# Expanding layer B's bias rows from the second pair of layer A on, and moving their last four transfers in SyncE's queue

## The chip, the cores and the metric

The kernel runs on one core of a Trainium2 chip. A core has TensorE (matmuls, PE in the profile, with its weight loads shown apart as PEld), VectorE (DVE), ScalarE (ACT), GpSimd (POOL) and SyncE (SP), which issues the DMA transfers here; the transfers run on 16 DMA engines. The metric is the time of one execution on the device in microseconds; lower is better.

## The reference

A block of two layers over 512 tokens of width 1024, 16 heads of 64. Each layer normalises x, multiplies it by one large weight matrix, mixes tokens, multiplies by silu of a gate and by an output matrix, and adds the result to x.

```python
for i in range(DEPTH):                      # DEPTH = 2
    hn = rms_norm(x, norm_gain[i])
    if i % 2 == 0:
        y = mixer_a(hn, a_w_in, a_w_out, a_q_gain, a_k_gain, t5_bias)
    else:
        y = mixer_b(hn, b_w_in, b_w_out, b_q_gain, b_k_gain, b_rpb)
    x = x + y
```

Layer A's mixer is attention over three dilated windows, whose outputs are merged by their softmax denominators; layer B's is attention of each token to its neighbours on an 8 x 64 grid. Both add a learned bias to the scores. Layer B's:

```python
bias = col_bias[:, row_idx].transpose(0, 2, 3, 1, 4)
logits = jnp.einsum('bhcqd,bhrcjd->bhcqrj', qr, kr) + bias
logits = jnp.where(col_valid[:, :, None, :], logits, NEG_INF)
p = jax.nn.softmax(logits...)
out = jnp.einsum('bhcqrj,bhrcjd->bhcqd', p, vr)
```

The bias depends on the distance of a query and a key in rows and columns, not on their places, so a table of 15 x 31 numbers for a head has to be spread out into one row for each query.

## The kernel before, in words

Float32 is kept by splitting every weight and activation into two parts (wh and wl, hn_h and hn_l) and summing three matmuls for each product (mm3). Weights stream in: wraw loads (L199, 512 KB each) go through SyncE's queue, ScalarE casts each to wh (L141), and VectorE or GpSimd subtracts for wl (L147, in split).

Layer A works on heads in eight pairs, hc = 0 to 7 in the code. While TensorE projects pair hc + 1 (main_a), the attention of pair hc (attn_a) is slipped in between, in two halves, u = 0 and u = 1. Each half forms scores (tiles called log) in four PSUM banks, takes exponentials, and VectorE transposes P in blocks into a tile tr (L905). A transfer writes tr to DRAM (td, L914) and four transfers read it back in order into pt (L918): that is P^T. The first half's reads fill half of pt, the second half's the rest. The products P^T V (weigh, tiles called o) follow once for the pair, in the first half of the next pair's attention; they need all eight reads. They take their two PSUM banks from the same four that the scores use, in turn, so pair 5's products use the banks of the first two score tiles of pair 6. The queries and keys of a pair make a similar trip through DRAM (qd, L716; qt, L723), and so does V (vd, L638; vv, L642). For pair 7 there is no such trip; pair 6's projection leaves the gate to later, so pair 5's second half has fewer matmuls behind it than that of other pairs.

The order on TensorE is written out by hand; the other engines' instructions follow the order in which the code emits them, or a scheduler's. What is to be issued at a later place is handed to later_on (L248) with a delay, counted in a running estimate of TensorE's time; tick emits it when the estimate gets there. So a transfer's place in SyncE's queue comes from such a delay. SyncE issues in order: what stands behind an issue that waits, waits too.

Layer A's bias for a pair is loaded by bias_a (tiles e, L877), a pair ahead. Layer B's bias is prepared during layer A by bias_rows (L465), which is called at the end of the first half of pair 2: it loads the table (rp, L468), GpSimd negates it (L469) and lays a copy with a border of large numbers (lb, L471 and L472), and two transfers write these to DRAM (gb_d, lb_d, L473 and L474). Fourteen transfers (spread_out, L486) expand the rows into ex_d, and four (in_order, L490, 640 KB each) copy them into the order in which layer B's bias_b reads them (eb_d). All eighteen are handed to later_on, 10500 apart from 30000 on.

Of the kernel before, what the change touches and what calls it, by code (L numbers as in the profile page):

```python
# [59 lines left out]
def tile_hybrid_encoder(  # L60
# [187 lines left out]
    def later_on(delay, job):  # L248

        timers.append((clock[0] + delay, job))  # L250
        timers.sort(key=lambda t: t[0])
# [123 lines left out]
    def row_scale(ssq):  # L375

        rsqrt(nc.vector, rs_n, ssq, 4, 1.0 / D)
# [28 lines left out]
    def gains():  # L406
        nc.sync.dma_start(hg, head_gain)
        nc.gpsimd.tensor_copy(ng.rearrange("p l k -> p (l k)"), x_ng[:, : 2 * KT])
        for i, (a, b) in enumerate(((0, 3), (1, 4), (2, 5), (6, 7))):
            m = nc.vector.scalar_tensor_tensor(  # L410
                gk[:, i : i + 1], hg[:, a : a + 1], -SCALE, hg[:, b : b + 1], op0=ALU.mult, op1=ALU.mult
            )
            tc.keep_in_program_order(m)

    def scales_a():
        pa = spread()
        nc.scalar.mul(trj(rs_half), to_trj(pa), 0.5)

    def norm(layer, k, xk):

        g = (ng if layer else x_ng[:, : 2 * KT].rearrange("p (l k) -> p l k", l=2))[:, layer, k : k + 1]
        h, l = hn_h[:, k, :], hn_l[:, k, :]
        nc.scalar.activation(h, xk, AF.Copy, scale=g)  # L423
        return nc.vector.scalar_tensor_tensor(l, xk, g, h.bitcast(F32), op0=ALU.mult, op1=ALU.subtract)

    def square_a(k):
        nc.scalar.activation(x_of(k), x_of(k), AF.Square)

    def row_sums(ssq):

        pk = bank("pk")
        for t in range(4):
            matmul(pk[:, t : t + 1], ssq[:, P * t : P * t + P], ones.bitcast(F32)[:, 0:1], start=True, stop=True)
        return pk[:, 0:4]

    def bias_lines():

        t5 = wk.tile([16, LINE], F32, tag="tr", name="t5", bufs=1)
        tc.keep_in_program_order(nc.sync.dma_start(t5, t5x))
        mk = wk.tile([16, LINE], F32, tag="q12", name="mk", bufs=1)  # L440
        nc.sync.dma_start(mk, maskc)
        nc.vector.tensor_sub(mk, mk, t5)
        nc.sync.dma_start(line_d[:, :384], mk[:, :384])
        nc.sync.dma_start(lines_d.rearrange("h g c -> h (g c)"), mk[:, 384:])

        def spread_out(dst, src):
            tc.keep_in_program_order(nc.sync.dma_start(dst, src))

        line = lambda o, *dims: bass.AP(line_d.tensor, line_d.offset + o, [[448, 16], *dims])
        fars = lambda o, *dims: bass.AP(lines_d.tensor, lines_d.offset + o, [[448, 32], *dims])  # L450
        far = l12_d.rearrange("h g r c -> (h g) r c")
        jobs = [
            (l0_d[:, 32 * j + 8 * s : 32 * j + 8 * s + 8, :], line(127 - j - 4 * s, [-16, 8], [1, 256]))
            for j in range(4)
            for s in range(4)
        ]
        jobs += [
            (far[:, 8 * s : 8 * s + 8, 56 * k : 56 * k + 56], fars(64 * (3 - s + k) + 7, [-1, 8], [1, 56]))
            for s in range(4)
            for k in range(4)  # L460
        ]
        for n, job in enumerate(jobs):
            later_on(3000 + 500 * n, partial(spread_out, *job))

    def bias_rows():  # L465

        rp = wk.tile([P, 248], F32, tag="eg", name="rp")
        tc.keep_in_program_order(nc.sync.dma_start(rp, rpb))  # L468
        nc.gpsimd.tensor_scalar(rp, rp, -1.0, None, op0=ALU.mult)  # L469
        lb = wk.tile([P, 376], F32, tag="eg", name="lb")  # L470
        nc.gpsimd.memset(lb, BIG)  # L471
        nc.gpsimd.tensor_copy(lb[:, 15 * 8 : 31 * 8], rp[:, 7 * 8 : 23 * 8])  # L472
        nc.sync.dma_start(gb_d, rp)  # L473
        nc.sync.dma_start(lb_d, lb)  # L474

        far, near = (lb_d, 376), (gb_d, 248)
        jobs = [(2 * W5 + W5 * n, W5, far, 120) for n in range(4)]
        jobs += [(o, 32, far, 24) for o in (0, W5, 7 * W5 - 32, 8 * W5 - 32)]
        jobs += [(32, 32, near, 216), (64, 96, near, 120), (W5 + 32, P, near, 88)]
        jobs += [(6 * W5, P, near, 56), (7 * W5, 96, near, 56), (7 * W5 + 96, 32, near, 24)]  # L480

        def spread_out(o, n, src, at):
            t, width = src
            dst = bass.AP(ex_d.tensor, ex_d.offset + o, [[4 * EB, P], [EB, 4], [1, n]])
            src = bass.AP(t.tensor, t.offset + at, [[width, P], [-8, 4], [1, n]])
            tc.keep_in_program_order(nc.sync.dma_start(dst, src))  # L486

        def in_order(c):
            dst = eb_d.rearrange("h (c r) x -> c h r x", c=4)[c]
            tc.keep_in_program_order(nc.sync.dma_start(dst, ex_d[:, c].rearrange("(h r) x -> h r x", h=16)))  # L490

        jobs = [partial(spread_out, *job) for job in jobs] + [partial(in_order, c) for c in range(4)]
        for n, job in enumerate(jobs):
            later_on(30000 + 10500 * n, job)

    st = {}
    pq = wk.tile([P, 4096], F32, tag="pt", name="pt", bufs=1)
# [373 lines left out]
    def bias_a(hc):  # L871
        e0 = wk.tile([P, 2, 256], F32, tag="e0", name="e0")
        e12 = wk.tile([P, 4, 224], F32, tag="e12", name="e12")
        hs = slice(2 * hc, 2 * hc + 2)

        def load(dst, src):
            tc.keep_in_program_order(nc.sync.dma_start(dst, src))  # L877

        load(e0, l0_d[hs].rearrange("h p c -> p h c"))
        for j in range(4):  # L880
            load(e12[32 * j : 32 * j + 32], l12_d[hs].rearrange("h g r c -> r (h g) c"))
        return e0, e12
# [471 lines left out]
    def side():  # L1354
        for k in range(KT):
            norm(0, k, x_of(k))
            if k:
                square_a(k - 1)
            stamp["na", k] = 0
            if k == 4:  # L1360
                gains()
            yield 1000
        square_a(KT - 1)
        for k in range(1, KT):
            yield 1300
            nc.vector.tensor_add(x_of(0), x_of(0), x_of(k))
        yield 1500
        row_scale(row_sums(x_of(0)))
        yield 2500
        bias_lines()  # L1370
        later_on(21000, lambda: st.__setitem__(("e", 0), bias_a(0)))
        yield 2500
        scales_a()
        first_out()
        stamp["rs", "a"] = 0
        halves = []
        for hc in range(NHC):
            if hc < NHC - 1:
                yield from q_a(hc)
                if hc:  # L1380
                    yield from halves.pop(0)
                yield from st.pop(("land", hc))()
                half = attn_a(hc)
                for v in half:
                    if v == "half":
                        if hc == 2:
                            bias_rows()
                        halves.append(half)
                        break
                    yield v  # L1390
            else:
                gap[0] = cycle((500, 500, 700))
                yield from halves.pop(0)
                yield from chain(q_a(hc), k_a(hc))
                yield from attn_a(hc)
        yield from residual(xg, 0)
        yield from residual(xg, 4)
        stamp["ya", KT - 1, "y"] = 0
        yield "wait", ("x", KT - 1), 800
        for f in range(KT):  # L1400
            square_b(f)
            yield 600
        yield 4500
        row_scale(row_sums(st.pop("ssq")))
        stamp["rs", "b"] = 0
        yield 5000
        nc.scalar.mul(rs_half, spread(), 0.5)
        stamp["rs", "all"] = 0
        for job, hc, delay in B_PLAN:
            yield "wait", ("b", "start"), delay  # L1410
            if job == "scores":
                yield from side_b(hc)
                continue
            if hc == NHC - 1:
                yield "wait", ("back", hc), 0
                yield from residual(xm_d, 0)
            yield "wait", ("back", hc), 3500
            if hc == NHC - 2:
                stamp["yb", "turned"] = 0
            pending.pop(0)()  # L1420
            if hc == NHC - 1:
                stamp["yb", "last"] = 0
            yield
            if hc == NHC - 1:
                yield from residual(xm_d, 4)

    run(main(), side())


# [101 lines left out]
```

## Time and profile before

| | |
|---|---|
| time, median of 3 runs | 808.53 us (807.92 to 809.21) |
| the profiled execution | 808.45 us |
| its span, first to last instruction | 806.7 us |
| TensorE busy | 798.6 us (99%) |
| VectorE, ScalarE, GpSimd busy | 526.6, 442.6, 222.2 us |
| mean granted clock of TensorE | 0.996 |
| moved by DMA | 174.76 MB, 217 GB/s on average |
| the rows of layer B's bias, expanded (L486) | issued from 258.2 to 401.2 us |
| their four transfers into read order (L490) | issued from 412.6 to 454.1 us |
| layer B's first read of them (L889) | 561.2 us |

All of a profile's times are from one execution; a time that stands alone is counted from the span's start. A row of a timeline begins with the start and the duration, then the engine, the line, the operation, what is written and read, and a count; in brackets stands how long the engine was idle before it and what the profile takes for the releaser, the event that ended the wait. SPq marks an issue by SyncE: its row is the time of issuing, not of the transfer. How long a transfer took to land, from its issue on, stands in the rows of DMA issues, with its size. The windows view gives the busy time of every engine in a stretch, the granted clock of TensorE (1.00 is full), and the busy share of the 16 DMA engines. The busy times of matmuls include a modelled end.

### The profile page before, as it was taken

The page shows a single profiled execution, that of the slowest core. Times are in us where ns is not written, and L with a number is a line of the kernel's source. Part 1 is how long each engine was busy: PE and PEld are TensorE (multiplying, and loading weights), DVE is VectorE, ACT ScalarE, POOL GpSimd, SP SyncE. Part 2 cuts the span into 40 slices and gives each one's busy share as a digit, 9 for nine tenths or more (in the row PEclk, how much of TensorE's full clock was granted, in tenths as well). Part 3 has the DMA queues.
Part 4 walks back from the last instruction along what each step waited for, and adds up shares of the span by engine and source line. Part 5 has one row for each costly group of instructions (what it writes and reads, how often), then busy time and mean ns, then how long its engine had stood idle before and what let it go on. Part 6 is the DMA issues. An engine that isn't in the chain of part 4 may idle for free.

```text
span 806.7 us, 17749 instructions
## 1 busy us (share of the span) xinstructions
PE 798.6 (99%) x6718; PEld 656.0 (81%) x6718; DVE 526.6 (65%) x1409; ACT 442.6 (55%) x933; POOL 222.2 (28%) x351
## 2 busy tenths in 40 slices
PE   9999999999999999999999989999999999999998
PEld 7888888888888888888888778888888888887887
DVE  7474575676676577577467647547664887896744
ACT  7442745745745745744754655635435665657721
POOL 2242432432441431532532322211220405020010
PEclk9999999999999999999999989999999999999999
DMA  8479578877887987967987966157646797899454
GB/s 291 151 208 264 157 222 240 239 209 208 262 221 210 297 238 225 288 198 226 287 247 225 308 205 184 32 181 221 159 154 197 208 242 217 215 259 287 153 153 176
DMA packets 97526, 174.76 MB, mean 217 GB/s; under 512 B 16608, under 2 KB 52592, under 8 KB 97440
## 3 DMA queue, kind: packets, MB, share of 16 engines
q1 hardware_dynamic: 97296, 173.36, 73.4%
q8 instruction: 53, 0.87, 0.5%
q10 hardware_dynamic: 144, 0.26, 0.1%
q14 instruction: 33, 0.27, 0.1%
HBM read 130.98 MB, written 50.86 MB: 225 GB/s over the span
## 4 chain that ended last, share of the span: by engine, by line
PE 87%; DMA 6%; DVE 4%; ACT 2%; issue 1%; POOL 0%; SPq 0%; POOLq 0%; DVEq 0%
PE acc L235 77%; PE o L235 4%; PE log L235 4%; DMA wraw<-in_w 3%; DMA qt<-qd 1%; DVE wl L147 1%; PE tp L239 1%; DMA qd<-rawq 1%; DVE rawq L333 1%; DMA vv<-bd 1%; ACT p L1294 0%; ACT wh L141 0%; POOL wl L147 0%; DVE na L128 0%; DVE rawq L586 0%
## 5 line engine op out<-in xcount | busy, mean ns | idle before, releaser
L235 PE MATMUL acc<-wh,hn_h 128*128 128x512 f32 x704 | 277.4, 395 | 0.2 <-ACT hn_h L423 0.2
L235 PE MATMUL acc<-wl,hn_h 128*128 128x512 f32 x704 | 273.8, 390 | 0.4 <-POOL wl L147 0.4
L235 PE MATMUL acc<-wh,hn_l 128*128 128x512 f32 x704 | 273.7, 389 | 0.0
L141 ACT CAST wh<-wraw 128x512 fp32r<-128x512 f32 (+1 forms) x258 | 157.7, 614 | 197.0 <-PE acc L235 166.0
L147 DVE TENSOR_TENSOR wl<-wraw,wh 128x512 fp32r<-128x512 f32 (+2 forms) x187 | 138.1, 739 | 152.9 <-ACT wh L141 151.1
L147 POOL TENSOR_TENSOR wl<-wraw,wh 128x512 fp32r<-128x512 f32 (+1 forms) x72 | 96.6, 1341 | 229.0 <-ACT wh L141 181.9
L235 PEld LDWEIGHTS acc<-wh,hn_h 128*128 128x128 f32 x704 | 132.1, 188 | 31.5 <-issue 3.8
L235 PEld LDWEIGHTS acc<-wh,hn_l 128*128 128x128 f32 x704 | 132.1, 188 | 28.0
L235 PEld LDWEIGHTS acc<-wl,hn_h 128*128 128x128 f32 x704 | 132.4, 188 | 27.6 <-POOL wl L147 1.1
L313 POOL TENSOR_TENSOR sq<-rawq 128x256 f32<-128x256 f32 (+1 forms) x82 | 59.6, 735 | 126.1 <-ACT rawq L549 114.1
L235 PE MATMUL acc<-y,wh 128*128 128x512 f32 (+1 forms) x272 | 81.5, 383 | 0.0
L997 ACT ACTIVATE p<-p,mn 128x512 f32<-128x512 f32 (+1 forms) x64 | 44.9, 702 | 60.1 <-DVE mn L986 60.1
L235 PE MATMUL acc<-hn_h,wh 128*128 128x512 f32 x192 | 75.9, 395 | 0.1
L235 PE MATMUL acc<-hn_h,wl 128*128 128x512 f32 x192 | 74.8, 390 | 0.0
L235 PE MATMUL acc<-hn_l,wh 128*128 128x512 f32 x192 | 74.8, 390 | 0.0
L314 DVE TENSOR_REDUCE ss<-sq 128x4 f32<-128x256 f32 (+1 forms) x96 | 47.6, 505 | 32.4 <-POOL sq L313 32.0
L235 PEld LDWEIGHTS acc<-y,wh 128*128 128x128 f32 x272 | 48.8, 188 | 9.2 <-issue 0.6
L235 PE MATMUL acc<-y,wl 128*128 128x512 f32 (+1 forms) x136 | 51.4, 378 | 0.0
L333 DVE TENSOR_TENSOR rawq<-rawq,rs 128x256 f32<-128x256 f32 (+1 forms) x96 | 47.0, 551 | 2.2 <-POOL rs L133 1.9
L905 DVE STREAM_TRANSPOSE tr<-p 128x512 f32<-128x512 f32 x56 | 38.9, 706 | 11.4 <-ACT p L821 11.4
L549 ACT ACTIVATE rawq<-acc,rs_n 128x512 f32<-128x512 f32 (+1 forms) x76 | 46.1, 614 | 0.5
L821 ACT ACTIVATE p<-p,mn 128x512 f32<-128x512 f32 (+1 forms) x64 | 44.5, 702 | 2.1 <-DVE mn L820 2.1
(140 smaller groups left out, 912.4 us busy)
## 6 DMA issues: line engine op xcount, KB each, us to landing
wraw<-in_w SPq DMA_DIRECT2D x120, 512.0 KB, 5.7
td<-tr SPq DMA_DIRECT2D x14, 1024.0 KB, 7.9
pt<-td SPq DMA_DIRECT2D x56, 256.0 KB, 4.8
qd<-rawq SPq DMA_DIRECT2D x7, 1536.0 KB, 6.9
qt<-qd SPq DMA_DIRECT2D x28, 384.0 KB, 6.4
tdb<-tb SPq DMA_DIRECT2D x8, 768.0 KB, 5.4
pt<-tdb SPq DMA_DIRECT2D x32, 192.0 KB, 5.8
eb<-eb_d SPq DMA_DIRECT2D x32, 160.0 KB, 5.2
```

The lines of the kernel that those rows point to most:

```text
L141: nc.scalar.copy(h, raw)
L147: eng.tensor_sub(l, raw, h.bitcast(F32))
L235: nc.tensor.matmul(o, l, r, **kw)
L239: nc.tensor.transpose(o, i, ident)
L313: nc.gpsimd.tensor_mul(to, v, v)
L314: nc.vector.tensor_reduce(ss[:, i * ns : (i + 1) * ns], sq.rearrange("p (a b) -> p a b", b=64), axis=AX.X, op=ALU.add)
L333: m = nc.vector.tensor_mul(v, v, by)
L549: nc.scalar.activation(dst, src, AF.Copy, scale=rs_n[:, i : i + 1])
L821: nc.scalar.activation(pr, pr, AF.Copy, scale=mn[:, 3:4])
L905: nc.vector.transpose(dst, src[:, :n].rearrange(order, b=4, k=32, **({"g": 2} if apart else {})))
L997: nc.scalar.activation(row, row, AF.Exp, bias=mn[:, 1:2], scale=-1.0, accum_out=mn[:, 2:3])
```

## The change

bias_rows is called a pair sooner, at the end of pair 1's first half. The fourteen transfers that expand rows start at 20000 instead of 30000 behind that call and keep their spacing. The four transfers into read order no longer follow them in the same list: they are kept, and two each are handed to later_on at the ends of the first halves of pairs 4 and 5, 9000 and 12500 behind. Nothing is added or removed.

```diff
         def in_order(c):
             dst = eb_d.rearrange("h (c r) x -> c h r x", c=4)[c]
             tc.keep_in_program_order(nc.sync.dma_start(dst, ex_d[:, c].rearrange("(h r) x -> h r x", h=16)))
 
-        jobs = [partial(spread_out, *job) for job in jobs] + [partial(in_order, c) for c in range(4)]
         for n, job in enumerate(jobs):
-            later_on(30000 + 10500 * n, job)
+            later_on(20000 + 10500 * n, partial(spread_out, *job))
+        st["rows"] = [partial(in_order, c) for c in range(4)]
...
                     if v == "half":
-                        if hc == 2:
+                        if hc == 1:
                             bias_rows()
+                        if hc in (4, 5):
+                            for n in range(2):
+                                later_on(9000 + 3500 * n, st["rows"].pop())
                         halves.append(half)
                         break
```

The order of instructions on TensorE, VectorE and ScalarE stays as it was. On SyncE's queue, pair 5's second half read as follows before, from the issue behind qd on (vd, vv: the trip of V; wraw: weights; e: layer A's bias of the next pair; a count at a row's end is of equal issues in a row):

```order
L490 DMA eb_d<-ex_d 16x8x1280
L638 DMA vd<-vv 128x4x128
L199 DMA wraw<-in_w 128x1024
L723 DMA qt<-qd 32x4x768 x4
L642 DMA vv<-vd 32x4x128 x4
L914 DMA td<-tr 128x4x512
L490 DMA eb_d<-ex_d 16x8x1280
L199 DMA wraw<-in_w 128x1024 x2
L877 DMA e_5201<-l_d 128x2x256
L877 DMA e_5202<-l_d 32x4x224 x4
L490 DMA eb_d<-ex_d 16x8x1280
L918 DMA pt<-td 32x4x512 x4
```

Now the same stretch reads:

```order
L638 DMA vd<-vv 128x4x128
L199 DMA wraw<-in_w 128x1024
L723 DMA qt<-qd 32x4x768 x4
L642 DMA vv<-vd 32x4x128 x4
L914 DMA td<-tr 128x4x512
L199 DMA wraw<-in_w 128x1024 x2
L877 DMA e_5202<-l_d 128x2x256
L877 DMA e_5203<-l_d 32x4x224 x3
L918 DMA pt<-td 32x4x512 x4
L877 DMA e_5203<-l_d 32x4x224
```

Three transfers into read order are gone from before the four reads of P^T, and one load of layer A's bias now stands behind them. In the first half of pair 5 SyncE's queue held one of the four among the reads:

```order
L914 DMA td<-tr 128x4x512
L918 DMA pt<-td 32x4x512
L490 DMA eb_d<-ex_d 16x8x1280
L918 DMA pt<-td 32x4x512 x2
L199 DMA wraw<-in_w 128x1024
L918 DMA pt<-td 32x4x512
L199 DMA wraw<-in_w 128x1024 x2
```

Now there are two, and pair 4's first half has two in the same way:

```order
L914 DMA td<-tr 128x4x512
L918 DMA pt<-td 32x4x512 x3
L199 DMA wraw<-in_w 128x1024
L490 DMA eb_d<-ex_d 16x8x1280
L918 DMA pt<-td 32x4x512
L490 DMA eb_d<-ex_d 16x8x1280
L199 DMA wraw<-in_w 128x1024 x2
```

They stand behind the third and the fourth of the first half's reads. On GpSimd's queue, in the first half of pair 1, there was this (wl: the split of weights; sq: squares for the norm of heads; y: layer A's output in parts):

```order
L133 TENSOR_TENSOR rs<-rs,na 128x16
L147 TENSOR_TENSOR wl<-wraw,wh 128x512 x2
L313 TENSOR_TENSOR sq<-rawq 128x4x4x32 x2
L147 TENSOR_TENSOR wl<-wraw,wh 128x512
L861 TENSOR_TENSOR y<-gt,y 128x512
```

Now there is:

```order
L133 TENSOR_TENSOR rs<-rs,na 128x16
L147 TENSOR_TENSOR wl<-wraw,wh 128x512
L471 MEMSET lb 128x376
L469 TENSOR_SCALAR rp<-rp 128x248
L472 COPY lb<-rp 128x128
L147 TENSOR_TENSOR wl<-wraw,wh 128x512
L313 TENSOR_TENSOR sq<-rawq 128x4x4x32 x2
```

The three operations on the table of biases stand between two splits of weights, where they stood in pair 2 before. The transfer of rp stands in SyncE's queue right behind the td of pair 1's first half, and the write of gb_d, which waits for GpSimd, behind it.

## The prediction

> Pairs are counted as in the code, hc = 0 to 7.
>
> **What bounds the kernel now.** I read the page's busy shares first, then the table of busy time by windows, then TensorE's timeline in the one window that is not full, then SyncE's timeline ahead of that place and the landing of single transfers.
>
> ```profile
> span 806.7 us, 17749 instructions
> PE 798.6 (99%) x6718; PEld 656.0 (81%) x6718; DVE 526.6 (65%) x1409; ACT 442.6 (55%) x933; POOL 222.2 (28%) x351
> ```
>
> TensorE is busy 798.6 of 806.7 us, and the change takes no matmul away, so all it can win is idle time of TensorE (8.1 us) and time at a lowered clock. The windows show where that lies (columns: stretch, its length, busy us of PE, PEld, DVE, ACT, POOL with counts, granted clock, share of the 16 DMA engines, GB/s):
>
> ```profile
> 0.00:10.00 10.00, 8.91 (x29) 6.88 (x30) 5.00 (x10) 6.64 (x11) 1.07 (x9) 1.00 0.79 290
> 220.00:230.00 10.00, 10.00 (x153) 8.42 (x152) 6.31 (x13) 3.42 (x7) 1.80 (x3) 1.00 0.55 178
> 405.00:430.00 25.00, 25.00 (x306) 20.56 (x305) 19.14 (x38) 9.64 (x16) 8.53 (x8) 1.00 0.68 199
> 430.00:468.00 38.00, 34.69 (x254) 28.13 (x257) 24.28 (x75) 23.42 (x45) 10.70 (x11) 0.97 1.01 302
> 460.00:470.00 10.00, 6.69 (x88) 5.50 (x90) 5.93 (x18) 5.00 (x10) 1.68 (x2) 0.80 1.02 319
> 465.90:472.70 6.80, 6.28 (x121) 5.81 (x122) 0.49 (x1) 0.82 (x2) 1.26 (x1) 0.50 0.78 299
> ```
>
> Away from the start and the end, TensorE has one hole, in 460 to 470: 3.31 us idle, and behind it 6.80 us at a granted clock of 0.50. TensorE's timeline names the instruction (in brackets the idle time before it and the releaser):
>
> ```profile
> 465.92 0.69 PE L235 MATMUL o<-pt,rawk 64*64 64x128 f32 x4 [2.80 <-DVE tr L905]
> 467.11 2.50 PE L235 MATMUL o<-pt,rawk 64*64 64x128 f32 x54 [0.51 <-DMA wraw<-in_w]
> 472.21 0.75 PE L235 MATMUL acc<-wh,hn_h 128*128 128x512 f32 x1
> ```
>
> These are the P^T V products of pair 5. They were due at 465.92 - 2.80 = 463.1. The releasers named are not the true ones. SyncE's timeline (the issues) and the landing of single transfers (last column, us from issue) tell what was late:
>
> ```profile
> 430.17 0.38 SPq L716 DMA_DIRECT2D qd<-rawq  x1
> 430.59 0.53 SPq L490 DMA_DIRECT2D eb_d<-ex_d  x1
> 443.04 0.38 SPq L914 DMA_DIRECT2D td<-tr  x1
> 445.72 0.52 SPq L490 DMA_DIRECT2D eb_d<-ex_d  x1
> 454.10 0.52 SPq L490 DMA_DIRECT2D eb_d<-ex_d  x1
> 455.32 4.83 SPq L918 DMA_DIRECT2D pt<-td  x4
> ...
> 458.84 0.30 SPq L918 DMA_DIRECT2D pt<-td  x1
> ```
>
> ```profile
> qd<-rawq SPq DMA_DIRECT2D x1, 1536.0 KB, 6.4
> eb_d<-ex_d SPq DMA_DIRECT2D x1, 640.0 KB, 8.3
> ...
> td<-tr SPq DMA_DIRECT2D x1, 1024.0 KB, 9.9
> ...
> eb_d<-ex_d SPq DMA_DIRECT2D x1, 640.0 KB, 8.4
> ...
> pt<-td SPq DMA_DIRECT2D x1, 256.0 KB, 6.9
> ...
> pt<-td SPq DMA_DIRECT2D x1, 256.0 KB, 7.7
> ```
>
> The rows are in the order of issue; the last two are the third and the fourth read of P^T. The third (458.84 + 6.9) landed at 465.7, and TensorE started at 465.92; the fourth (issued at 459.2, as a row below shows) landed at 466.9, and TensorE went on at 467.11. The reads go to partitions 0, 64, 32, 96 in turn, so the products over partitions 0 to 63 need the first and the third, the others the second and the fourth. That fits both waits.
>
> **What the stall costs.** 2.80 + 0.51 = 3.31 us of idle time, and 6.80 us at half clock, in which half the work is lost: 3.40 us. Together 6.7 us.
>
> [...] By the rows here, a wait that is left over may cost 3.4 us more; that touches the second rival, not the sum.
>
> **What the change takes from that place.** Three of the four transfers into read order (L490, 640 KB) stand ahead of the four reads there. From 430 to 468 the DMA engines' share is 1.01, so what stands ahead delays what stands behind by its own transfer time. The one at 430.59 landed at 438.9, and the one ahead of it, qd, at 430.17 + 6.4 = 436.6: 2.3 us. The one at 445.72 landed at 454.1, td ahead of it at 452.9: 1.2 us, but the two ran interleaved. I take 2.3 us for each, since it was measured with nothing between; the other end is 1.2. Three make 6.9 us (3.6 at the low end). The fourth read then lands at 466.9 - 6.9 = 460.0 (463.3) and the third at 458.8 (462.1), against 463.1 when they are due: 3.1 us early, or 0.2 late at the low end.
>
> Pair 4 gives a second estimate, without such a transfer between td and the reads (the middle row is the tile's own view; its last row gives min, median, max to landing):
>
> ```profile
> 380.07 0.57 SPq L914 DMA_DIRECT2D td<-tr  x1
> ...
> L918 SPq DMA_DIRECT2D pt<-td x4: 318/426/1494, 391.4 to 393.8; - x4
> ...
> DMA to landing us min/median/max: 3.5/4.1/5.1
> ...
> 407.05 2.72 PE o L235 x120
> ```
>
> ```profile
> L918 SPq DMA_DIRECT2D pt<-td x4: 302/307/960, 455.3 to 459.2; - x4
> ```
>
> From td to the last landing it took 393.8 + 5.1 - 380.07 = 18.8 us there, 23.8 in pair 5 (443.04 to 466.9). With 18.8 from the same td the last read lands at 461.9, 1.2 us early, and td itself can only come sooner with one L490 transfer less ahead of it. Both estimates say that the stall goes. Hence 6.7 us of gain, all of it or nearly none if the reads are a few us late.
>
> What is late next there: in pair 4 nothing (its reads landed 8 us before the products at 407.05); in pair 5 the reads themselves, 1 to 3 us early.
>
> **What it adds elsewhere.** The four L490 transfers now stand in pairs 4 and 5, two each, among the reads of the first half (u = 0), which are wanted only by the products at the end of the second half. In pair 5 one stood there already; a second adds 2.3 us. The last load of that stretch:
>
> ```profile
> 423.64 0.35 SPq L199 DMA_DIRECT2D wraw<-in_w  x1
> ...
> wraw<-in_w SPq DMA_DIRECT2D x1, 512.0 KB, 3.6
> ```
>
> It landed at 427.2, and the next transfer, qd, was issued at 430.17: 2.9 us of an empty queue, which hold the 2.3. With that cover gone, up to 2.3 us of the 3.1 would be used up and the stall would still not return. The window 405 to 430 has a share of 0.68, so there is room, and TensorE is busy 25.00 of 25.00 us in it. In pair 4 two are added (4.6 us) and two smaller ones leave; the reads among which they stand have 40 us to go. I cost both at nothing, with 0 to 0.5 us as bounds.
>
> The fourteen transfers that expand rows (L486, at most 320 KB each) are due one pair and 10 us sooner, in pairs 1 to 3 instead of 2 to 4. By SyncE's order pairs 2, 3 and 4 carried four to six of them each, TensorE did not wait, and pair 4's reads were 8 us early. One costs no more than an L490 transfer of twice its size, 2.3 us. Pair 1 gets five where it had none: I take nothing, 0 to 0.3.
>
> GpSimd's three small operations on rp and lb move from pair 2 to pair 1, where GpSimd again waits for the load of rp with a split of weights (L147) behind it:
>
> ```profile
> 160.85 2.72 PE o L235 x120
> ...
> 222.56 2.72 PE o L235 x120
> ```
>
> ```profile
> 228.14 0.84 POOL L469 TENSOR_SCALAR rp<-rp 128x248 f32<-128x248 f32 x1 [9.51 <-DMA rp<-in_rpb]
> ```
>
> ```profile
> 159.77 0.38 SPq L914 DMA_DIRECT2D td<-tr  x1
> ...
> td<-tr SPq DMA_DIRECT2D x1, 1024.0 KB, 8.0
> ```
>
> In pair 2 rp came 5.6 us after the products in its first half began (228.14 against 222.56), and TensorE was busy 10.00 of 10.00 us. In pair 1 rp stands behind td, which landed at 159.77 + 8.0 = 167.8, so rp comes 7 us after the products at 160.85: 1.4 later than in pair 2. GpSimd is 28% busy; I take nothing, at most those 1.4 us. SyncE waits too, at the write of gb_d behind rp (L473); queued behind it are reads of the first half and loads of weights, as in pair 2.
>
> **The sum.** The profiled execution took 808.45 us (span 806.7 and 1.75 around it), 0.08 below the median 808.53. 808.45 - 6.7 + 0 = 801.75; I predict 801.8.
>
> **Rivals.** (1) *Slower: the wait moves to pair 1.* GpSimd holds a split of weights behind rp; if rp landed so late that TensorE stood still for over 3.3 us there, the wait and its half clock (3.4) would eat the whole gain. With 5 us the time would be 801.8 + 8.4 = 810.2. For it: the place is real, and rp stands behind 1 MB. Against it: pair 2 had the same wait of 9.51 us at no cost, and rp would have to come well over 3.3 us behind the 167.8 at which td lands. (2) *A shorter wait is left.* If a moved transfer gives back only its low end, the reads land 0.2 us late, and by pair 4's spacing they are 1.2 us early, so a spill of 2 to 3 us leaves about 1.2 us: 803.0 with the clock kept, 806.4 with half clock behind it. [...] (3) *No change.* The releaser named for the 2.80 us is a DVE transpose; were it the true one, moving transfers would do nothing: 808.4. Against it: the products write two PSUM banks that the first two score tiles held, and these were last read by
>
> ```profile
> 456.58 0.47 DVE L986 CUSTOM_DVE_ANT_1 p<-log,e,mn 128x256 f32<-128x256 f32 x1
> ...
> 456.98 0.48 DVE L986 CUSTOM_DVE_ANT_1 p<-log,e,mn 128x256 f32<-128x256 f32 x1
> ```
>
> six us before they were due, while both waits end with a landing of a read.
>
> **How the numbers follow.** Forecast (stall gone) 0.83; rival 2 0.10, most of it with the clock kept; rival 3 0.04; rival 1 0.03. The runs shown spread from 807.92 to 809.21, 0.6 on either side; a measurement of this kernel can tell about 0.2% (1.6 us) from no change. The low end is 801.8 - 0.6 - 0.4 (the rest of the small idle times) = 800.8. The high end takes in rival 2 up to a wait of 2.6 us at full clock: 804.4. Faster by over 0.2% means under 806.9: the forecast and rival 2, 0.93. Within 0.2%: rival 3, 0.04. Slower: rival 1, 0.03.
>
> **What would show it.** Right: no row of TensorE with idle time before the products of pair 5, the windows behind them at 1.00, TensorE's busy time lower (the half clock stretched it), the fourth read of pair 5 landing at 458 to 462 on the old time axis, no L490 transfer between qd and those reads. Wrong in size: the reads landing within 1 us of the products, or a granted clock under 1.00 somewhere behind a short wait. Wrong in kind: idle time before a product in pair 1 with GpSimd as its releaser, or the same 2.8 us with the reads long landed.

## The result, and the profile after

The changed kernel took 804.62 us (median of four runs, 803.70 to 805.53), the kernel before 808.75 beside it: a ratio of 0.995, 95% interval 0.9933 to 0.9967. The forecast was 801.8 with a range up to 804.4. So the change gains 4.1 us instead of the 6.9 that lie between 801.8 and 808.75, and 2.8 us are missing.

The page of the changed kernel's profiled execution, which took 803.7 us:

```profile
span 801.9 us, 17756 instructions
PE 795.2 (99%) x6718; PEld 653.0 (81%) x6718; DVE 527.2 (66%) x1409; ACT 442.1 (55%) x933; POOL 222.2 (28%) x351
```

TensorE's busy time fell by 3.4 us (798.6 to 795.2), which is what the half clock had cost. Its idle time fell by only 1.4 (8.1 to 6.7), though 3.31 us of it had stood at pair 5. The windows show both (columns as before):

```profile
180.00:200.00 20.00, 18.27 (x167) 14.31 (x166) 16.82 (x42) 9.21 (x19) 2.92 (x4) 1.00 0.75 227
405.00:430.00 25.00, 25.00 (x307) 20.56 (x305) 18.39 (x39) 11.52 (x20) 7.60 (x6) 1.00 0.72 234
455.00:470.00 15.00, 15.00 (x262) 12.62 (x246) 12.82 (x40) 8.33 (x18) 2.60 (x2) 1.00 0.98 248
465.90:472.70 6.80, 6.80 (x124) 5.60 (x119) 3.59 (x6) 4.36 (x8) 2.86 (x3) 1.00 0.67 242
```

At pair 5 TensorE is now busy all the time and the clock stays at 1.00; the two transfers in the first half (405 to 430) cost nothing. The fourth read of P^T came close, though. Its issue, its landing and the products in the changed kernel:

```profile
456.35 0.30 SPq L918 DMA_DIRECT2D pt<-td  x1
...
pt<-td SPq DMA_DIRECT2D x1, 256.0 KB, 8.2
...
464.92 1.57 PE L235 MATMUL o<-pt,rawk 64*64 64x128 f32 x64
```

It landed at 456.35 + 8.2 = 464.6, 0.4 us ahead of the products, where 3.1 had been forecast.

The missing time is elsewhere. The stretch from 180 to 200, in pair 1's second half, lost 1.73 us; the kernel before was busy there without a gap:

```profile
180.00:200.00 20.00, 20.00 (x176) 16.05 (x175) 14.56 (x35) 10.45 (x21) 3.28 (x6) 1.00 0.73 213
```

TensorE's timeline of that place in the changed kernel:

```profile
192.94 0.39 PE L235 MATMUL acc<-wl,hn_h 128*128 128x512 f32 x1
193.16 0.39 PE L235 MATMUL acc<-wh,hn_l 128*128 128x512 f32 x1
194.43 0.49 PE L235 MATMUL acc<-wh,hn_h 128*128 128x512 f32 x1 [0.87 <-ACT wh L141]
195.78 0.50 PE L235 MATMUL acc<-wl,hn_h 128*128 128x512 f32 x1 [0.85 <-POOL wl L147]
```

TensorE waited for a cast of weights and then for a split: 0.87 + 0.85 = 1.72 us. These two waits are called the hole of pair 1 below. Going back from that cast, engine by engine, one reaches GpSimd in pair 1's first half, 25 us earlier. GpSimd's timeline there, first before, then after:

```profile
165.20 1.59 POOL L147 TENSOR_TENSOR wl<-wraw,wh 128x512 fp32r<-128x512 f32 x1 [8.62 <-ACT wh L141]
168.69 1.04 POOL L313 TENSOR_TENSOR sq<-rawq 128x512 f32<-128x512 f32 x1 [1.90 <-ACT rawq L549]
170.60 1.04 POOL L313 TENSOR_TENSOR sq<-rawq 128x512 f32<-128x512 f32 x1 [0.86 <-ACT sq L311]
```

```profile
167.87 1.25 POOL L469 TENSOR_SCALAR rp<-rp 128x248 f32<-128x248 f32 x1 [11.14 <-DMA rp<-in_rpb]
169.19 0.29 POOL L472 COPY lb<-rp 128x128 f32<-128x128 f32 x1
169.44 1.29 POOL L147 TENSOR_TENSOR wl<-wraw,wh 128x512 fp32r<-128x512 f32 x1
170.69 1.04 POOL L313 TENSOR_TENSOR sq<-rawq 128x512 f32<-128x512 f32 x1
172.60 1.04 POOL L313 TENSOR_TENSOR sq<-rawq 128x512 f32<-128x512 f32 x1 [0.86 <-DVE ss L314]
```

GpSimd stood 11.14 us for rp, did the split that had queued behind it, and only then the squares of the queries and keys (sq, L313, needed for their norm): at 170.69 instead of 168.69. VectorE sums these squares (L314), scales the queries and keys by their norm (L333), and behind that in its queue works on the scores of pair 1's second half (L974). First before, then after:

```profile
169.77 1.45 DVE L314 TENSOR_REDUCE ss<-sq 128x8 f32<-128x512 f32 x2 [1.13 <-POOL sq L313]
...
180.03 2.50 DVE L333 TENSOR_TENSOR rawq<-rawq,rs 128x512 f32<-128x512 f32 x4
...
185.34 0.38 DVE L974 CUSTOM_DVE_ANT_0 p<-log,e 128x256 f32<-128x256 f32 x1
```

```profile
171.77 1.28 DVE L314 TENSOR_REDUCE ss<-sq 128x8 f32<-128x512 f32 x2 [3.34 <-POOL sq L313]
...
181.97 2.49 DVE L333 TENSOR_TENSOR rawq<-rawq,rs 128x512 f32<-128x512 f32 x4
...
187.27 0.38 DVE L974 CUSTOM_DVE_ANT_0 p<-log,e 128x256 f32<-128x256 f32 x1
```

All of this comes some two microseconds later (1.93 at L974). ScalarE takes the exponentials of those scores and divides them by their sums (L821), and the casts of weights stand behind these in its queue. Again before, then after:

```profile
190.62 1.32 ACT L821 ACTIVATE p<-p,mn 128x512 f32<-128x512 f32 x2
191.84 1.65 ACT L141 CAST wh<-wraw 128x512 fp32r<-128x512 f32 x3
```

```profile
192.54 1.32 ACT L821 ACTIVATE p<-p,mn 128x512 f32<-128x512 f32 x2
193.77 1.64 ACT L141 CAST wh<-wraw 128x512 fp32r<-128x512 f32 x3
```

The casts came 1.93 us later (191.84 to 193.77), or 2.1 counted from the start of pair 1's products, which was at 160.78 in the execution before and at 160.58 in this one. TensorE stood for 0.87 of these, so about 1.3 us had been slack (time by which the casts could be late at no cost). Then it stood 0.85 more for a split on GpSimd.

### The profile page after: what moved, and what is told of

It reads as the page before. It is cut to its first block, busy times and chain, and to the rows that moved or that the text cites. A ratio compares the mean times of both kernels' runs of the same rounds, so it can differ in the third digit from the quotient of the medians.

```text
span 801.9 us, 17756 instructions
## 1 busy us (share of the span) xinstructions
PE 795.2 (99%) x6718; PEld 653.0 (81%) x6718; DVE 527.2 (66%) x1409; ACT 442.1 (55%) x933; POOL 222.2 (28%) x351
## 4 chain that ended last, share of the span: by engine, by line
PE 71%; DVE 2%; ACT 1%; DMA 1%; issue 0%
PE acc L235 62%; PE log L235 4%; PE o L235 4%; PE tp L239 1%; DMA bd<-rawq 1%; DVE wl L147 0%; ACT p L1294 0%; ACT wh L141 0%; ACT p L1299 0%; ACT rawq L549 0%; DVE tb L1229 0%; DVE ss L314 0%; DVE rawq L742 0%; DVE rawq L333 0%; DVE gx L814 0%
## 5 line engine op out<-in xcount | busy, mean ns | idle before, releaser
L147 DVE TENSOR_TENSOR wl<-wraw,wh 128x512 fp32r<-128x512 f32 (+2 forms) x187 | 138.6, 742 | 150.3 <-ACT wh L141 148.4
L147 POOL TENSOR_TENSOR wl<-wraw,wh 128x512 fp32r<-128x512 f32 (+1 forms) x72 | 96.2, 1336 | 226.6 <-ACT wh L141 173.6
L313 POOL TENSOR_TENSOR sq<-rawq 128x256 f32<-128x256 f32 (+1 forms) x82 | 59.5, 734 | 125.6 <-ACT rawq L549 112.8
L314 DVE TENSOR_REDUCE ss<-sq 128x4 f32<-128x256 f32 (+1 forms) x96 | 47.6, 505 | 34.7 <-POOL sq L313 34.2
L333 DVE TENSOR_TENSOR rawq<-rawq,rs 128x256 f32<-128x256 f32 (+1 forms) x96 | 47.0, 550 | 2.2 <-POOL rs L133 1.9
L905 DVE STREAM_TRANSPOSE tr<-p 128x512 f32<-128x512 f32 x56 | 38.9, 706 | 11.4 <-ACT p L821 11.4
L821 ACT ACTIVATE p<-p,mn 128x512 f32<-128x512 f32 (+1 forms) x64 | 44.4, 701 | 2.1 <-DVE mn L820 2.1
```

The source lines that it names most:

```text
L147: eng.tensor_sub(l, raw, h.bitcast(F32))
L313: nc.gpsimd.tensor_mul(to, v, v)
L314: nc.vector.tensor_reduce(ss[:, i * ns : (i + 1) * ns], sq.rearrange("p (a b) -> p a b", b=64), axis=AX.X, op=ALU.add)
L333: m = nc.vector.tensor_mul(v, v, by)
L821: nc.scalar.activation(pr, pr, AF.Copy, scale=mn[:, 3:4])
L905: nc.vector.transpose(dst, src[:, :n].rearrange(order, b=4, k=32, **({"g": 2} if apart else {})))
```

## The experiments

Three readings of the new wait stood against each other. **A**: GpSimd's wait for rp holds the squares, as above. **B**: SyncE's wait at the write of gb_d (8.9 us in the changed kernel) holds reads and weights. **C**: the expansion's transfers (L486), now from pair 1 on, delay weights and V. Theory D, on the three transfers at pair 5, and E and F, on the clock, come further down; in the expectations of the two runs on those three transfers, theory A is another one, that each of them costs its own 2.2 us. Each timed kernel ran beside the kernel before, whose medians were 808.52 to 808.83 there; a ratio is to those runs.

**Load of rp earlier.** In the changed kernel the load is issued ahead of pair 1's attention; the three operations and the two writes are held in program order, so that they keep their places:

```diff
+                if hc == 1:
+                    load_rows()          # rp's tile and its transfer
                 half = attn_a(hc)
...
     def bias_rows():
-        rp = wk.tile([P, 248], F32, tag="eg", name="rp")
-        tc.keep_in_program_order(nc.sync.dma_start(rp, rpb))
+        rp = st.pop("rp")
```

> The changed kernel, with the load of rp alone put ahead: issued before pair 1's attention starts, so that it lands before GpSimd reaches L469; GpSimd's three operations and the two writes keep their places. Theory A (GpSimd waits for rp, and the squares L313 queued behind it reach VectorE 2 us late, then the exponentials, the casts and TensorE): the 1.72 us of idle time at 193.6 to 195.8 and the lowered clock of some executions go, 802.0 (801.7 to 802.4), granted clock 1.000 in all executions. Theory B (SyncE's wait at the write of gb_d holds reads and weights): also 802.0, the wait goes too. Theory C (the rows' transfers L486, now in pair 1, stand ahead of weights and V): no change, 804.6.

It took 801.70 us (801.62 to 801.79, five runs), ratio 0.9914 (0.9901 to 0.9927). GpSimd no longer waited, and the squares were back in time (line numbers are three higher from L468 on):

```profile
156.39 0.83 POOL L472 TENSOR_SCALAR rp<-rp 128x248 f32<-128x248 f32 x1
157.17 0.41 POOL L474 MEMSET lb<- 128x376 f32 x1
157.64 0.29 POOL L475 COPY lb<-rp 128x128 f32<-128x128 f32 x1
165.05 1.58 POOL L147 TENSOR_TENSOR wl<-wraw,wh 128x512 fp32r<-128x512 f32 x1 [7.12 <-ACT wh L141]
168.53 1.04 POOL L313 TENSOR_TENSOR sq<-rawq 128x512 f32<-128x512 f32 x1 [1.90 <-ACT rawq L552]
```

TensorE has no idle time in 150 to 215 there. The transfers of the rows are where the change puts them, so C falls. The move of one 124 KB load is worth 2.9 us against the changed kernel's 804.62.

**Only the four transfers moved.** Bias rows are called in pair 2 with the old delays, and the four are put into pairs 5 and 6, since their rows are expanded later than in the changed kernel:

```diff
-                        if hc == 1:
+                        if hc == 2:
                             bias_rows()
-                        if hc in (4, 5):
+                        if hc in (5, 6):
...
-            later_on(20000 + 10500 * n, partial(spread_out, *job))
+            later_on(30000 + 10500 * n, partial(spread_out, *job))
```

> The kernel before, with only the four transfers into read order moved: bias rows called in pair 2 as before, their fourteen transfers where they were, the four in the first halves of pairs 5 and 6, two each. Theory A and B: the stall of 6.7 us in pair 5 goes and nothing is added in pair 1: 802.0 (801.7 to 802.5), clock 1.000. Theory C: also 802.0. If instead the earlier expansion of the rows was needed for the gain (an emptier queue in pairs 4 and 5), part of the stall stays: 803 to 806.

It took 801.82 us (801.51 to 801.89), ratio 0.9914 (0.9902 to 0.9927). The last read of P^T and the products of pair 5, in SyncE's and TensorE's timelines and the landing:

```profile
452.53 0.30 SPq L918 DMA_DIRECT2D pt<-td  x1
```

```profile
pt<-td SPq DMA_DIRECT2D x1, 256.0 KB, 7.7
```

```profile
462.66 1.57 PE L235 MATMUL o<-pt,rawk 64*64 64x128 f32 x64
```

It landed at 452.53 + 7.7 = 460.2, 2.4 us ahead of the products. So the move of the four transfers gives the whole gain, and the earlier expansion was not needed for it.

**Only the call moved.** The kernel before with `if hc == 1` ahead of bias_rows, and all eighteen delays longer by one pair (56853), so that the transfers stay where they were.

> The kernel before, with only the call moved to pair 1: rp, the three operations of GpSimd and the two writes are in pair 1, and all eighteen transfers keep their old places by a delay that is one pair longer. Theory A and B: the old stall stays and the new wait of 1.7 us comes on top: 808.7 + 1.7 = 810.4, up to 812 with the clock lowered behind it too. Theory C: 808.7, since no transfer of the rows is in pair 1.

It took 811.80 us (810.77 to 813.49), ratio 1.0039 (1.0026 to 1.0052), 3.3 us slower than before. TensorE's timeline has the new wait and the old one:

```profile
194.50 0.49 PE L235 MATMUL acc<-wh,hn_h 128*128 128x512 f32 x1 [0.88 <-ACT wh L141]
195.85 0.50 PE L235 MATMUL acc<-wl,hn_h 128*128 128x512 f32 x1 [0.86 <-POOL wl L147]
```

```profile
469.46 0.69 PE L235 MATMUL o<-pt,rawk 64*64 64x128 f32 x4 [4.41 <-DVE tr L905]
470.45 2.50 PE L235 MATMUL o<-pt,rawk 64*64 64x128 f32 x54 [0.31 <-DMA pt<-td]
```

The hole in pair 1 is the changed kernel's, with no transfer of the rows near it. The old one was longer, 4.72 us instead of 3.31; why it grew is not shown.

**SyncE does not wait.** In the changed kernel only the two writes are handed on:

```diff
-        nc.sync.dma_start(gb_d, rp)
-        nc.sync.dma_start(lb_d, lb)
+        def write():
+            tc.keep_in_program_order(nc.sync.dma_start(gb_d, rp))
+            tc.keep_in_program_order(nc.sync.dma_start(lb_d, lb))
+        later_on(14500, write)
```

> The changed kernel, with only the two writes (gb_d, lb_d) handed on by 14500, so that SyncE doesn't wait for GpSimd ahead of the reads of P^T and the weights; GpSimd waits for rp as before. Theory A: no change, 804.6, with 1.7 us of idle time at the same place. Theory B: 802.0 and no idle time there. Theory C: 804.6.

It took 803.83 us (802.84 to 805.52), ratio 0.9941 (0.9929 to 0.9954), with the hole as it was:

```profile
194.52 0.49 PE L235 MATMUL acc<-wh,hn_h 128*128 128x512 f32 x1 [0.88 <-ACT wh L141]
195.87 0.50 PE L235 MATMUL acc<-wl,hn_h 128*128 128x512 f32 x1 [0.86 <-POOL wl L147]
```

B falls: it is not SyncE's wait.

**GpSimd's operations later.** The other way round: the load of rp stays behind td, and the three operations and two writes are put into a function that is handed to later_on with 14500.

> The changed kernel, with the load of rp where it is and GpSimd's three operations and the two writes handed on by 14500, so that they stand behind the squares and splits of weights of pair 1's first half. Theory A: rp has landed when GpSimd gets there, the squares are not held, no idle time: 801.8, as with the load moved ahead. Theory C: 804.6.

It took 801.89 us (801.74 to 802.00), ratio 0.9914 (0.9901 to 0.9928). The squares came at 168.69 again, and L469's operation (L472 here) ran at 179.89 without a wait. With the earlier load, this shows A from both sides.

**A longer wait for rp.** In the changed kernel one more transfer ahead of rp's:

```diff
+        pad = dr.tile([P, 1280], F32, name="pad")
+        tc.keep_in_program_order(nc.sync.dma_start(pad, xg.rearrange("p k s -> p (k s)")[:, :1280]))
         tc.keep_in_program_order(nc.sync.dma_start(rp, rpb))
```

> The changed kernel with one more transfer of 640 KB (part of an input, written to a scratch tensor that nothing reads) ahead of the load of rp in pair 1, so that rp lands some 2.2 us later. Theory A (what GpSimd waits for sets the hole): idle time of 1.7 + 2.2 = 3.9 us in pair 1, in the same two places; 805.9 at full clock, 809.3 if the clock is halved behind it, which is slower than the kernel before. Theory C (the rows' transfers): unchanged, 804.6.

It took 807.07 us (805.12 to 808.27, eleven runs), ratio 0.9981 (0.9972 to 0.9990). TensorE's timeline and the window behind it:

```profile
196.28 0.50 PE L235 MATMUL acc<-wh,hn_h 128*128 128x512 f32 x1 [2.50 <-ACT wh L141]
197.63 0.80 PE L235 MATMUL acc<-wl,hn_h 128*128 128x512 f32 x1 [0.85 <-POOL wl L147]
```

```profile
196.90:203.70 6.80, 6.07 (x14) 4.80 (x15) 3.19 (x3) 1.50 (x3) 2.03 (x2) 0.50 1.01 228
```

The squares began at 172.38, 1.69 later than in the changed kernel, and the first wait grew by 1.63 (0.87 to 2.50): one for one. GpSimd had rp 2.10 us later (169.97 instead of 167.87), near the 2.2 that were expected, but the negation took 0.84 us there instead of 1.25. So the squares came only 1.69 later, and 3.35 us stand where 3.9 were expected. In the profiled execution, the slowest of the eleven (808.27), the clock was halved for 6.8 us behind it.

**One and two of the three transfers at pair 5 moved.** The kernel before, with the last one or two taken out of the list and handed on in pair 6's first half:

```diff
+        st["rows"] = [jobs.pop() for _ in range(1)]     # or range(2)
...
+                        if hc == 6:
+                            for n in range(1):          # or range(2)
+                                later_on(9000 + 3500 * n, st["rows"].pop())
```

With two left:

> The kernel before, with one of the three transfers into read order taken from ahead of pair 5's last four reads (the one issued at 454.1) and put in pair 6's first half. With all three moved (the run that moved only the four) the last read landed at 460.2 instead of 466.9: 2.2 us each. Theory A (each transfer ahead costs its own 2.2 us): last read at 464.7, 1.6 us of idle time before pair 5's products (due at 463.1). Then 803.4 if the clock holds, 806.8 if it is halved for 6.8 us. Theory D (one that runs interleaved costs 1.2, so one moved brings little): last read at 465.7, 2.6 us of idle time, 804.4 at full clock, 807.8 with the clock halved.

807.17 us (803.79 to 809.01, eleven runs), ratio 0.9979 (0.9964 to 0.9994). With one left:

> The kernel before, with two of the three moved to pair 6's first half; the one issued at 430.6 stays. Theory A: last read at 462.4, 0.7 us ahead of the products: no idle time, 801.8. Theory D (1.2 each): last read at 464.5, 1.4 us of idle time, 803.2 or, with the clock halved, 806.6.

803.50 us (802.62 to 803.66), ratio 0.9931 (0.9919 to 0.9944). TensorE's waits, two left, then one left:

```profile
466.03 0.43 PE L235 MATMUL o<-pt,rawk 64*64 64x128 f32 x4 [2.77 <-DVE mn L821]
467.51 2.50 PE L235 MATMUL o<-pt,rawk 64*64 64x128 f32 x54 [1.04 <-DVE tr L906]
```

```profile
463.87 1.40 PE L235 MATMUL o<-pt,rawk 64*64 64x128 f32 x55 [0.42 <-DVE tr L906]
```

Neither 2.2 us for each nor D's 1.2 describes this. The last read landed at 467.3 with two left, 463.7 with one and 460.2 with none. The first of these is from the slowest execution of its run (809.01), whose reads were as late as before, so it doesn't stand for the median. The three together are worth 6.7 us, as costed. Taken one by one they are worth about 1.7, 3.9 and 1.4 by the ratios (0.9979, 0.9931 and 0.9914; the last is from the run that moved all four). Why the steps are unequal is not shown. The products start when a landing allows it: with two left, the third read landed at 465.8 and the fourth at 467.3, some 0.2 us ahead of the two rows. The profile names the transposes (L906, the L905 of the kernel before) or a reciprocal (L821) instead.

**Where some executions lose 1.5 us more.** The changed kernel's four runs fell into two groups: 803.70 and 804.08 with a granted clock of 1.000, 805.15 and 805.53 with 0.998. The median of 804.62 lies between them. Two more executions of the same kernel were profiled to see the second kind, with these expectations:

> The changed kernel once more, for the profile of an execution with a granted clock of 0.998 (two of the four timed ones had that, at 805.2 and 805.5; the profiled one had 1.000 and 803.7). Theory E: the clock falls behind the hole of pair 1, at 196 to 203, 3.4 us lost in a half of the cases or less. Theory F: it falls behind pair 5's products, whose last read landed only 0.3 us ahead of them in the profiled execution, and there is idle time there. If this one has a clock of 1.000 it tells nothing.

> The same as the run before it: a second look for an execution with a lowered clock. Theory E: window 196 to 203 below 1.00. Theory F: a window behind pair 5's products below 1.00, with idle time ahead.

Both had a clock of 1.000 (804.16 and 803.81) and told nothing on this. Then, on one chip, the changed kernel once more, and a version whose four transfers are put near the end of layer A:

```diff
-                        if hc in (4, 5):
-                            for n in range(2):
-                                later_on(9000 + 3500 * n, st["rows"].pop())
+                        if hc == 6:
+                            for n in range(4):
+                                later_on(42000 + 3500 * n, st["rows"].pop())
```

> The changed kernel, with the four transfers into read order taken out of pairs 4 and 5 altogether and put near the end of layer A, at about 510 to 520, where the queue is nearly empty (share 0.11 in 500 to 520 of the changed kernel). The call stays in pair 1, so the hole of 1.7 us there stays, and pair 5's reads land earlier than in the changed kernel. It tells where the executions at a granted clock of 0.998 lose 1.5 us. Theory E (behind the hole of pair 1): still two of six or so at 0.998, 805.3, the others 803.7. Theory F (at pair 5's products, when the last read comes late): all at 1.000, 803.6 to 803.9.

> The changed kernel once more, timed on the same chip as the run with the four transfers near the end of layer A. Theory E and F alike: some executions near 803.8 at a granted clock of 1.000, about one in three near 805.3 at 0.998. If the profile falls on one of the latter: Theory E wants the window 196 to 203 below 1.00, Theory F a window behind pair 5's products.

The version took 803.89 us (802.46 to 805.10), ratio 0.9944 (0.9931 to 0.9956); one of its five runs had 0.998. The changed kernel took 805.39 (802.56 to 805.65, six runs), ratio 0.9953 (0.9939 to 0.9967); five of six had 0.998, and the profile fell on one of these (805.65). Its windows:

```profile
196.70:200.10 3.40, 3.40 (x10) 2.61 (x9) 1.60 (x1) 0.00 (x0) 1.05 (x1) 0.50 1.05 226
```

```profile
466.00:473.00 7.00, 7.00 (x140) 5.92 (x139) 4.16 (x9) 4.76 (x8) 1.27 (x1) 1.00 0.78 276
```

The clock is halved for 3.40 us right behind the hole of pair 1 (1.70 us lost, against 1.5 between the means of the two groups), and full at pair 5: E, not F, in the one such execution profiled. Of the twelve executions of the changed kernel, seven had 0.998. The version's profiled execution had only one wait in pair 1, of 0.72 us, where 1.7 were expected to stay, and took 802.46. GpSimd's timeline fits theory A: it had rp at 167.38, 0.49 sooner than in the changed kernel, the negation took 0.84 us, and the squares began at 169.82 instead of 170.69. A smaller delay of the squares went with a smaller hole. The one execution of the changed kernel at 802.56 may be of this kind, which is not shown.

## Why the prediction was right in one half and wrong in the other

- **The stall of pair 5 and its price: right, with less to spare than forecast.** 6.7 us were costed; with nothing else changed the time fell from 808.52 to 801.82. The last read was forecast to land at 460.0, 3.1 us ahead of the products. It landed at 460.2, 2.4 ahead, when only the four were moved. In the changed kernel it was 0.4 ahead, and in three more profiles of the same kernel 0.2 behind the first of the products (at 804.16), 2.0 ahead (803.81) and 1.0 ahead (805.65). TensorE had no idle time there in any of the four, but with such margins this was partly luck. The sign "the reads landing within 1 us of the products" was seen; why they land closer than with the four transfers alone is not shown. That the products wait for reads and not for the named releaser holds too, since VectorE's work was not touched. Rivals 2 and 3 did not come.
- **2.3 us for each transfer ahead: right as a sum in one run, wrong as a rate.** Three were to give 6.9 us, and with only the four moved the last read landed 6.7 sooner. In the changed kernel it landed 0.4 us ahead of the products instead of 3.8 behind, a gain of only 4.2. The runs with one and two left show unequal steps.
- **The transfers put into pairs 4 and 5, and the expansion a pair sooner, at nothing: right.** With the load of rp early, all of them are in place and the time is 801.70.
- **GpSimd's wait at nothing, at most 1.4 us: wrong.** This is the step that failed. The landing of rp was right (forecast 167.8; GpSimd began at 167.87). What failed is who waits behind it. The prediction named only the split of weights (L147) behind the wait, sought a cost in TensorE's idle time at the same place (220 to 230), and took GpSimd's 28% of busy time for room. Behind that split stand the squares (L313), and through them VectorE, ScalarE and the casts of the next half. The argument that pair 2 had the same wait of 9.51 us at no cost compared lengths of waits, where ends were wanted. The term of 1.4 us did compare ends, but not with the time at which the work behind is due. From the negation of rp to the squares GpSimd takes 0.84 + 0.29 + 1.30 = 2.4 us, as the rows below show. In pair 1 the squares are due at 168.69, 7.84 behind the start of the products at 160.85, so rp is wanted 5.4 behind them. In pair 2 it came 5.58 behind. In pair 1 it was forecast for 7.0 behind, 1.6 late. The measured delay was larger: the squares came at 170.69 instead of 168.69, while the products began 0.2 us sooner in this execution, so 2.2 late; the negation alone took 1.25 us in pair 1 where it had taken 0.84 in pair 2. "1.4 later than in pair 2" was therefore nearly all delay, and the engines behind it spread what was left of it into two waits.

GpSimd's timeline in pair 2 of the kernel before, which had been there to read:

```profile
228.14 0.84 POOL L469 TENSOR_SCALAR rp<-rp 128x248 f32<-128x248 f32 x1 [9.51 <-DMA rp<-in_rpb]
229.04 0.29 POOL L472 COPY lb<-rp 128x128 f32<-128x128 f32 x1
229.29 1.30 POOL L147 TENSOR_TENSOR wl<-wraw,wh 128x512 fp32r<-128x512 f32 x1
230.54 1.49 POOL L313 TENSOR_TENSOR sq<-rawq 128x512 f32<-128x512 f32 x1
```

There the squares follow the split without a gap: the wait had no slack left. Against the products of their pair, these squares are 0.14 us later than in the kernel with rp loaded early, where GpSimd does not wait in pair 2.

- **The bound had no clock in it.** The second rival said that a wait may cost the clock as well; the term for pair 1 did not take this over. The missing 2.8 us are 1.72 of idle time and, in seven of twelve executions, by their mean clock of 0.998, some 1.7 of half clock (3.40 us at 0.50 in the one profiled): 801.8 + 1.7 = 803.5 without it and 805.2 with it, where eleven of the runs stood at 803.7 to 804.2 and 805.2 to 805.7, and one at 802.56. That a wait left over keeps the clock, as the forecast's high end of 804.4 takes it for 2.6 us and the larger part of rival 2's chance takes it too, was the author's estimate, and no profiled run shows the term. The profiles show a clock of 1.00 behind waits of 0.42 and 0.72 us and, in three of four, behind 1.72 in two parts; they show 0.50 behind 1.7 in the fourth and behind 2.50 + 0.85.
- **Rival 1** had the place right (pair 1, GpSimd, rp) and its chance too low. It priced only a wait long enough to make the kernel slower; a short one that eats part of the gain was no case of its own. Even with rp 2 us later the kernel was not slower than before (0.9981).

The two versions without the wait, with the earlier load of rp (801.70) and with GpSimd's operations later (801.89), beat both kernels, as does the move of the four transfers alone (801.82).

## What to carry to other kernels

When a step that waits is moved, write down every instruction queued behind it on its engine, up to the first one with real slack, and follow each through the engines that consume it; the nearest one is not always the one that is due first. That a wait of the same length was free elsewhere says nothing: compare when it ends with when the work behind it is due, at the old place and at the new. A load that something will wait for is issued early, not together with the work that needs it.

## What the runs showed of the hardware

In the windows shown, a granted clock of 0.50 lasted 3.40 us (changed kernel at 805.65, from 196.70 to 200.10) and 6.80 us (kernel before, from 465.90 to 472.70; longer wait for rp, from 196.90 to 203.70). The same two waits, 0.87 to 0.89 and 0.84 to 0.85 us, stand in four profiles of the changed kernel: behind three of them (803.70, 804.16 and 803.81) the clock stayed at 1.00, behind the fourth (805.65) it was halved for 3.40 us. By the mean clock, seven of its twelve executions had 0.998, as the fourth had. A single wait of 0.42 us (one transfer left at pair 5), or of 0.72 (the four transfers near the end of layer A), had no halved clock behind it in the execution profiled: 1.00 in 460 to 473 and in 195 to 210. So here a wait of 1.7 us in two parts, within 2.2 us, cost either itself or twice itself, and the kernel has two groups of times. Why the clock was halved behind one of the four and not behind the others, no run shows.
